# Attention scores from stacked queries and doubled keys, and other ties for row sums and splits, in a decoder trunk kernel

## The chip, the core and the metric

The kernel runs on one core of one Trainium2 chip. Its time is device microseconds, as the median of a few runs; smaller is better. Time before the change: 688.33 us, median of three runs (688.19 to 689.62).

## What is computed

One decoder layer over 512 tokens of 1024 channels, in fp32: an adaLN-modulated RMSNorm, a combined input projection, two causal token mixers (sliding-window attention with 8 query heads on 2 key heads, differential attention with 4 heads of two maps), their branch projections, gates, an output projection, and a gated MLP with a small convolution. The change touches the scores of the two mixers:

```python
qb = q.reshape(b, nb, BLOCK, SWA_KV_HEADS, SWA_GROUP, d)
scores = jnp.einsum('bnqkgd,bnskd->bnkgqs', qb, kb).astype(jnp.float32) * (d ** -0.5)   # sliding window
...
scores = jnp.einsum('bqhmd,bshmd->bhmqs', qblk, k).astype(jnp.float32) * scale          # differential
...
mod = cs @ w_ada[l] + b_ada[l]      # adaLN: shift, scale, gate, twice
```

A head has 64 channels, so a score sums over 64.

## The kernel before

**Split operands.** TensorE (PE) multiplies numbers in the type fp32r. To keep fp32 accuracy each operand is held as a high part (rounded to fp32r by a ScalarE, ACT, copy) and a low part (the rest, by a VectorE, DVE, subtraction): `split` (L101), `split_pair` (L95) for weights, `evac` (L404) for a projection that leaves PSUM. A product is three products: high by high, high by low, low by high (`mm3`, L105). A weight goes through a raw buffer (`raw_tile`, L90, four of them, shared by everything that is loaded so) and a ring of three split buffers (`WB`).

**Scores.** The two sub-heads that are worked on together (two key heads of the window, two maps of a differential head) lie in partitions 0 to 63 and 64 to 127 of the same tile. Their scores are three products each over half of the array's rows, written pairwise by `mm3_rows` (L110): `swa_scores` (L500) for a pair of window heads and two 128-query blocks, `diff_scores` (L609) for one or two blocks of a differential head. The key width is 128 or 256 in the window and 128 to 512 in the differential head. A DVE instruction then adds the distance penalty and takes the row maximum (L527, L634), the softmax runs on ACT and DVE (`swa_softmax` L533, `diff_softmax` L640), and PE transposes the probabilities (`swa_transpose` L553, `diff_transpose` L657) before it multiplies them by the values.

**Order.** In attention the order of PE is written out by hand (`manual_schedule` at L450). Between the pieces of attention `fill(n)` (L459) issues n steps of other projections; a step is three products of 512 columns and a unit has eight or four. `prefetch` (L454) loads and splits the weights of the next units. `fill` also counts ticks, and at the ticks in `ADA_AT` (L30) it takes one row of `ada_rows` (L706): load 128 rows of `w_ada`, and on DVE multiply and sum them (L711) into `late_mod`. There are 32 such rows; the first eight columns feed the gate of the output projection, the others later parts. `issue_after(x)` puts instructions behind x on x's engine, without a wait of their own. The row sums stand behind the last score reduction (`behind_dve`). On DVE and ACT a planner orders the instructions by priority; `high_priority` lifts the softmax.

**Before and after attention.** The first projection sums over eight slices k (`mm_k`, L347) into eight PSUM banks: key (0), window queries 0 and 1 (1, 2), window value (5), values (3, 4, 6, 7). The last slice takes all eight first products, then the other two of each. After attention come the gates and branch products (`add_gate_d` L860, `add_merge` L869, whose weight pairs `wbd` share one buffer, L874), the output projection with rows `wo` (`load_rows` L930, L966), and the MLP, whose first weights are split early (`prep` L1038, L1055).

Of the kernel before, what the change touches and what calls it, by code (L numbers as in the profile page):

```python
# [29 lines left out]
ADA_AT = set(range(20, 150, 8)) | set(range(180, 300, 5))  # L30
# [3 lines left out]
SWA_FILL = (0, 3, 6, 2, 2, 2, 2, 3)  # L34
# [7 lines left out]
def kernel(  # L42
# [50 lines left out]
    lows = [None]  # L93

    def split_pair(raw, shape, name):  # L95
        hi = wp.tile(shape, F32R, tag="whi", bufs=WB, name=name + "_h")
        lo = wp.tile(shape, F32R, tag="wlo", bufs=WB, name=name + "_l")
        lows[0] = split(hi, lo, raw)
        return hi, lo

    def split(hi, lo, src):  # L101
        nc.scalar.copy(hi, src)
        return nc.vector.tensor_sub(lo, src, hi.bitcast(F32))
# [5 lines left out]

    def mm3_rows(groups):  # L110
        for a, b, start, stop in ((0, 0, True, False), (0, 1, False, False), (1, 0, False, True)):
            for o, lhs, rhs in groups:
                nc.tensor.matmul(o, lhs[a], rhs[b], start=start, stop=stop)  # L113
# [233 lines left out]
    def mm_k(k, part):  # L347
# [53 lines left out]
    ka = big.tile([P, 2, S], F32R, tag="kvA", name="ka")  # L401
    outa = [big.tile([P, 4, S], F32R, tag=f"out{g}", name=f"outa{g}") for g in "hl"]

    def evac(hi, lo, src, scale=None):  # L404
        if scale is None:
            nc.scalar.copy(hi, src)
            return nc.vector.tensor_sub(lo, src, hi.bitcast(F32))
# [16 lines left out]

    keep_v(3)
    evac(qa[:, 1, 0], qa[:, 1, 1], acc[2], qsc[:, 1:2])
    keep_v(4)
    nc.scalar.copy(vaT, acc[5])
# [23 lines left out]
    current, tick, behind_dve = [], [0], [None]  # L452
# [6 lines left out]
    def fill(n):  # L459
        for _ in range(n):  # L460
# [20 lines left out]
            if tick[0] in ADA_AT:  # L481
# [18 lines left out]
    def swa_scores(i, n0):  # L500
# [9 lines left out]
        sps = [sbank(f"sw{i}_{n0}_{j}", (P, 2, 256)) for j in range(2)]  # L510
        for n in (n0, n0 + 1):
# [11 lines left out]
        for n in (n0, n0 + 1):  # L523
# [1248 lines left out]
```

## Time and profile before

| | before |
|---|---|
| median of three runs | 688.33 us |
| the profiled execution | 686.36 us |
| its span, first to last instruction | 684.6 us |
| PE busy | 673.5 us |
| PE weight loads busy | 589.6 us |
| DVE busy | 556.8 us |
| ACT busy | 383.5 us |
| GpSimd (POOL) busy | 65.9 us |
| granted TensorE clock | 0.998 |

A line of the timeline reads: start in us, duration in us, engine, line, operation, output and inputs, shapes, count; in square brackets the idle time of the engine before it and what ended it. A matmul's shape gives first the part of the array that it uses (128*128 or 64*128). A matmul's duration holds its way through the array; matmuls overlap, so the cost of one in a sequence is the distance from its start to the next start. PEld is the load of the weights of a matmul. In the chain of work the times are those distances, with a count. SPq is the queue that issues most DMAs. In the list of waits a line gives the total, the number of times and the longest.

### The profile page before, as it was taken

How to read it: one execution, taken by the hardware profiler on the slowest of the kernel's cores; microseconds unless marked ns; L12 is line 12 of the kernel's file. 1: busy time of each engine (PE TensorE's matmuls, PEld its weight loads, DVE VectorE, ACT ScalarE, POOL GpSimd, SP SyncE). 2: the span in 40 equal slices, each digit the busy share in tenths (PEclk: the TensorE clock that was granted, in tenths of full speed). 3: DMA queues.
4: the chain of work that ended last, by engine and by line, in shares of the span. 5: the costliest groups of instructions: out<-in, count | busy, mean ns of one | idle time of the engine just before them, and what ended most of it. 6: DMA issues, size and time to landing. Idle time of an engine off the chain costs nothing.

```text
span 684.6 us, 10929 instructions
## 1 busy us (share of the span) xinstructions
PE 673.5 (98%) x4117; PEld 589.6 (86%) x4117; DVE 556.8 (81%) x1036; ACT 383.5 (56%) x678; POOL 65.9 (10%) x74
## 2 busy tenths in 40 slices
PE   8999999999999999999999999999999999999995
PEld 7887777778788888788799999999999998888884
DVE  5996867778775677773689998888888999979997
ACT  6676756454554332441588565666555666656665
POOL 2000000000100000000020110111110003540300
PEclk9999999999999999999999999999999999999999
DMA  9952224454363667347672989787866658996903
GB/s 355 417 214 79 94 85 149 145 170 150 97 183 94 200 236 245 119 161 226 197 124 83 215 226 209 177 200 186 204 170 184 152 171 198 199 204 187 165 1 124
DMA packets 71077, 119.68 MB, mean 175 GB/s; under 512 B 3952, under 2 KB 47728, under 8 KB 71024
## 3 DMA queue, kind: packets, MB, share of 16 engines
q1 hardware_dynamic: 52960, 95.04, 41.8%
q0 software_dynamic: 17776, 23.60, 21.1%
q8 instruction: 32, 0.52, 0.3%
q10 hardware_dynamic: 288, 0.34, 0.2%
q14 instruction: 21, 0.17, 0.1%
HBM read 116.87 MB, written 2.10 MB: 174 GB/s over the span
## 4 chain that ended last, share of the span: by engine, by line
PE 78%; DMA 9%; DVE 8%; issue 3%; ACT 1%; DVEq 0%; POOLq 0%; ACTq 0%
PE up L1098 32%; PE dc L1701 11%; DMA ra<-in_w_ada_t_dram 4%; PE av L345 3%; DMA s_t<-in_w_up_dram 2%; PE pga L106 2%; PE aqa L342 2%; PE pga L107 2%; PE pga L108 2%; PE sd L113 1%; PE pk L106 1%; PE pq L106 1%; DVE ra L711 1%; PE pk L108 1%; PE pq L108 1%
## 5 line engine op out<-in xcount | busy, mean ns | idle before, releaser
L1098 PE MATMUL up<-t,m_whi 128*128 128x256 f32 x512 | 93.1, 283 | 0.0
L1098 PEld LDWEIGHTS up<-t,m_whi 128*128 128x128 f32 x512 | 79.9, 192 | 0.0
L1098 PE MATMUL up<-t,m_wlo 128*128 128x256 f32 x256 | 72.4, 283 | 0.0
L1098 PE MATMUL up<-bh,p_whi 128*128 128x256 f32 x232 | 65.7, 283 | 0.0
L1098 PE MATMUL up<-bl,p_whi 128*128 128x256 f32 x232 | 65.7, 283 | 0.0
L1098 PE MATMUL up<-bh,p_wlo 128*128 128x256 f32 x232 | 65.7, 283 | 0.0
L711 DVE CUSTOM_DVE_ANT_0 ra<-ra,csb 128x1024 f32<-128x1024 f32 x32 | 39.0, 1220 | 16.5 <-DMA ra<-in_w_ada_t_dram 16.5
L1098 PEld LDWEIGHTS up<-t,m_wlo 128*128 128x128 f32 x256 | 49.2, 192 | 0.0
L1098 PEld LDWEIGHTS up<-bh,p_whi 128*128 128x128 f32 x232 | 44.5, 192 | 0.0
L1098 PEld LDWEIGHTS up<-bl,p_whi 128*128 128x128 f32 x232 | 44.5, 192 | 0.0
L1098 PEld LDWEIGHTS up<-bh,p_wlo 128*128 128x128 f32 x232 | 44.5, 192 | 0.0
L1004 POOL DMA_DIRECT2D s<-in_w_up_dram x21 | 27.0, 1365 | 158.1 <-DMA s<-in_w_up_dram 128.9
L1032 ACT CAST m_whi<-s 128x1024 fp32r<-128x1024 f32 x31 | 32.5, 1048 | 15.7 <-DVE s L1026 9.1
L1036 DVE TENSOR_TENSOR m_wlo<-s,m_whi 128x1024 fp32r<-128x1024 f32 x31 | 37.7, 1217 | 1.3 <-ACT m_whi L1032 1.3
L1098 PE MATMUL up<-t,p_whi 128*128 128x256 f32 x176 | 32.2, 283 | 0.0
L648 ACT ACTIVATE sd<-sd,dmx 128x128 f32<-128x128 f32 (+3 forms) x32 | 17.8, 557 | 23.9 <-DVE dmx L646 23.2
L1098 PEld LDWEIGHTS up<-t,p_whi 128*128 128x128 f32 x176 | 27.4, 192 | 0.1
L144 POOL TENSOR_TENSOR r<-ms,mhalf 128x4 f32<-128x4 f32 x4 | 5.1, 1276 | 219.1 <-DVE dls L652 149.6
L1032 ACT CAST p_whi<-wa 128x1024 fp32r<-128x1024 f32 x18 | 18.8, 1043 | 12.6 <-PE up L1098 9.0
L1036 DVE TENSOR_TENSOR p_wlo<-wa,p_whi 128x1024 fp32r<-128x1024 f32 x18 | 22.0, 1222 | 4.0 <-ACT p_whi L1032 3.3
L1105 ACT ACTIVATE gT<-a,cols 128x512 f32<-128x512 f32 x22 | 17.6, 813 | 13.3 <-DVE a L1140 13.0
L1098 PE MATMUL up<-t,p_wlo 128*128 128x256 f32 x88 | 24.9, 283 | 0.0
(517 smaller groups left out, 2018.8 us busy)
## 6 DMA issues: line engine op xcount, KB each, us to landing
ra<-in_w_ada_t_dram SPq DMA_DIRECT2D x32, 512.0 KB, 3.4
wa<-in_w_up_dram SPq DMA_DIRECT2D x22, 512.0 KB, 4.4
s<-in_w_up_dram SPq DMA_DIRECT2D x21, 512.0 KB, 4.6
s<-in_w_up_dram POOLq DMA_DIRECT2D x21, 512.0 KB, 6.6
adaw<-in_w_ada_t_dram SPq DMA_DIRECT2D x15, 512.0 KB, 9.6
a<-in_w_up_dram SPq DMA_DIRECT2D x11, 512.0 KB, 4.9
b<-in_w_down_dram SPq DMA_DIRECT2D x10, 512.0 KB, 4.1
w<-in_w_first_dram SPq DMA_DIRECT2D x8, 512.0 KB, 9.9
```

The source lines that it names most:

```text
L106: nc.tensor.matmul(o, lh, rh, start=start, stop=False)
L107: nc.tensor.matmul(o, lh, rl, start=False, stop=False)
L108: nc.tensor.matmul(o, ll, rh, start=False, stop=stop)
L345: nc.tensor.matmul(acc[i], ht[:, t : t + P], wts[k][w][:, S:], start=start, stop=stop)
L648: nc.scalar.activation(pm[m], pm[m], AF.Exp, bias=mx[:, m : m + 1], scale=slope, accum_out=lsum[:, m : m + 1])
L711: nc.vector.tensor_tensor_reduce(r, r, csb, 1.0, 0.0, ALU.mult, ALU.add, late_mod[:, idx : idx + 1])
L1004: nc.gpsimd.dma_start(dst, upblock(*blk), accum_op=ALU.add)
L1032: nc.scalar.copy(W[J, name][0], R[J, SRC[name]])
L1036: nc.vector.tensor_sub(lo, R[J, SRC[name]], hi.bitcast(F32))
L1098: nc.tensor.matmul(o[u], w[:, k, cu], b[:, k], start=name in ("p1", "m5", "p2") and k == 0 and x == 0, stop=k == 3 and x == 2, skip_group_ ...
L1105: nc.scalar.activation(grow(j), av[J][:, u], AF.Identity, bias=cv[:, 66 + j : 67 + j], scale=cv[:, 44 + j : 45 + j])
L1701: nc.tensor.matmul((bank2[u] if o is None else o)[:, sl], a[:, q, cu], b[:, q, sl], start=first_mm and x == 0, stop=last_mm and x == 2, sk ...
```

## The change

Queries are stacked: for each sub-head one tile of 128 partitions holds the high part in the sub-head's own 64 partitions and the low part in the other 64. Keys are doubled: the high part in both halves of one tile, the low part in both halves of another. A score is then two products over all 128 rows: stacked query by doubled high key, and by doubled low key. (The sum gains low by low, which the three products left out.) The scores are written sub-head by sub-head.

Beside that: the last slice of the first projection finishes its banks one after the other, value 3 and key first; the order of ACT and DVE right behind it is written out by hand; one filler step comes ahead of the first scores and two, not three, behind them; the value transposes come four filler steps later. The row sums of `ada_rows` no longer come at ticks 20 to 148 but behind the last instruction of a softmax (`ada_behind`), and from tick 180 on at every fifth tick behind the last two splits (`recent`). `wbd` alternates between two buffers. The first `wo` row stands behind the last two splits, and the early split of `p2` behind the last `wo` split on ACT too.

```diff
-ADA_AT = set(range(20, 150, 8)) | set(range(180, 300, 5))
+ADA_LATE = 180
+ADA_EVERY = 5
...
-SWA_FILL = (0, 3, 6, 2, 2, 2, 2, 3)
+VA_AT = 5
+SWA_FILL = (1, 2, 6, 2, 2, 2, 2, 3)
...
+    casts, lows, recent = [None], [None], [None, None]
...
-        lows[0] = split(hi, lo, raw)
+        casts[0], lows[0] = split(hi, lo, raw)
+        recent[:] = recent[1:] + lows
...
-
-    def mm3_rows(groups):
-        for a, b, start, stop in ((0, 0, True, False), (0, 1, False, False), (1, 0, False, True)):
-            for o, lhs, rhs in groups:
-                nc.tensor.matmul(o, lhs[a], rhs[b], start=start, stop=stop)
...
         elif part == 0:
-            for i in range(8):
-                product(k, i, 0)
-        elif part == 1:
-            for i in range(8):
-                product(k, i, 1)
-                product(k, i, 2)
+            for i in (3, 0, 1, 5, 2, 4, 6, 7):
+                for p in range(3):
+                    product(k, i, p)
...
-    ka = big.tile([P, 2, S], F32R, tag="kvA", name="ka")
+    ka = big.tile([P, 2, 2, S], F32R, tag="kvA", name="ka")
+    lower, upper = slice(0, 64), slice(64, P)
...
-    def evac_q(i):
-        evac(qa[:, i, 0], qa[:, i, 1], acc6[i], qsc[:, i : i + 1])
-
-    evac(ka[:, 0], ka[:, 1], acc[0])
-    evac(qa[:, 0, 0], qa[:, 0, 1], acc[1], qsc[:, 0:1])
+    halves = ((lower, upper), (upper, lower))
+
+    def stack(dst, src, scale, js=(0, 1), soon=True):
+        with tc.high_priority(offset=HP) if soon else ExitStack():
+            sc = [scale if isinstance(scale, float) else scale[own] for own, _ in halves]
+            for j in js:
+                own = halves[j][0]
+                nc.scalar.activation(dst[own, j], src[own], AF.Copy, scale=sc[j])
+            for j in js:
+                own, other = halves[j]
+                nc.vector.scalar_tensor_tensor(
+                    dst[other, j], src[own], sc[j], dst[own, j].bitcast(F32), ALU.mult, ALU.subtract
+                )
+
+    def double(dst, src):
+        with tc.high_priority(offset=HP):
+            for j, (own, _) in enumerate(halves):
+                nc.scalar.copy(dst[own, j, 0], src[own])
+            for j, (own, _) in enumerate(halves):
+                nc.vector.tensor_sub(dst[own, j, 1], src[own], dst[own, j, 0].bitcast(F32))
+            for j, (own, other) in enumerate(halves):
+                nc.scalar.copy(dst[other, j], dst[own, j])
...
+    man = ExitStack()
+    man.enter_context(tc.manual_schedule(engines={nc.vector.engine, nc.scalar.engine}))
     keep_v(3)
-    evac(qa[:, 1, 0], qa[:, 1, 1], acc[2], qsc[:, 1:2])
+    for j, (own, other) in enumerate(halves):
+        for to in (own, other):
+            nc.scalar.copy(ka[to, j, 0], acc[0][own])
+    for j, (own, _) in enumerate(halves):
+        nc.vector.tensor_sub(ka[own, j, 1], acc[0][own], ka[own, j, 0].bitcast(F32))
+    stack(qa[:, 0], acc[1], qsc[:, 0:1])
+    for j, (own, other) in enumerate(halves):
+        nc.scalar.copy(ka[other, j, 1], ka[own, j, 1])
+    nc.scalar.copy(vaT, acc[5])
+    man.close()
+    stack(qa[:, 1], acc[2], qsc[:, 1:2], soon=False)
     keep_v(4)
-    nc.scalar.copy(vaT, acc[5])
     keep_v(6)
     keep_v(7)
...
-    current, tick, behind_dve = [], [0], [None]
...
-            if tick[0] in ADA_AT:
+            if tick[0] >= ADA_LATE and tick[0] % ADA_EVERY == 0:
                 next(ada, None)
...
+        sps = {j: sbank(f"sw{i}_{n0}_{j}", (P, 2, 256)) for j in range(2)}
+        for j, n in ((j, n) for j in range(2) for n in (n0, n0 + 1)):
             w = P if n == 0 else 2 * P
             k0 = max(0, n - 1) * P
             qs, ks = slice(n * P, (n + 1) * P), slice(k0, k0 + w)
-            mm3_rows([
-                (
-                    sps[j][:, n - n0, :w],
-                    [qa[64 * j : 64 * j + 64, i, b, qs] for b in range(2)],
-                    [ka[64 * j : 64 * j + 64, b, ks] for b in range(2)],
-                )
-                for j in range(2)
-            ])
-        for n in (n0, n0 + 1):
-            w = P if n == 0 else 2 * P
-            for j in range(2):
+            for b in range(2):
+                nc.tensor.matmul(sps[j][:, n - n0, :w], qa[:, i, j, qs], ka[:, j, b, ks], start=b == 0, stop=b == 1)
+        for j in range(2):
+            for n in (n0, n0 + 1):
+                w = P if n == 0 else 2 * P
...
-                    behind_dve[0] = c.last
...
-                    nc.vector.tensor_scalar_mul(c.sb[n][:, j, :w], c.sb[n][:, j, :w], c.lsum[:, j, n : n + 1])
+                    c.end = nc.vector.tensor_scalar_mul(c.sb[n][:, j, :w], c.sb[n][:, j, :w], c.lsum[:, j, n : n + 1])
...
-            evac(qa[:, i, 0], qa[:, i, 1], o, qsc[:, i : i + 1])
+            stack(qa[:, i], o, qsc[:, i : i + 1])
...
-            t = heads[h] = ap.tile([P, 4, S], F32R, tag="qk", bufs=2, name=f"qk{h}")
+            t = heads[h] = ap.tile([P, 6, S], F32R, tag="qk", bufs=2, name=f"qk{h}")
...
-            evac(t[:, 0], t[:, 1], o, 2.0 ** (2 * h - 1))
+            stack(t[:, 0:2], o, 2.0 ** (2 * h - 1))
...
-            evac(t[:, 2], t[:, 3], o)
+            double(t[:, 2:6].rearrange("p (j b) s -> p j b s", b=2), o)
...
-            mm3_rows([
-                (
-                    sps[m],
-                    [t[64 * m : 64 * m + 64, b, n * P : (n + 1) * P] for b in range(2)],
-                    [t[64 * m : 64 * m + 64, 2 + b, :w] for b in range(2)],
-                )
-                for m in range(2)
-            ])
+            for m in range(2):
+                for b in range(2):
+                    nc.tensor.matmul(
+                        sps[m], t[:, m, n * P : (n + 1) * P], t[:, 2 + 2 * m + b, :w], start=b == 0, stop=b == 1
+                    )
...
-                    behind_dve[0] = nc.vector.tensor_tensor_reduce(
+                    nc.vector.tensor_tensor_reduce(
...
-            nc.vector.scalar_tensor_tensor(pm[0], pm[0], lsum[:, 0:1], pm[1], ALU.mult, ALU.add)
+            end = nc.vector.scalar_tensor_tensor(pm[0], pm[0], lsum[:, 0:1], pm[1], ALU.mult, ALU.add)
             probs[s] = pm[0]
+        return end
...
         with tc.high_priority(offset=HP):
-            end = evac(hi, lo, tp[:, : (n + 1) * P].rearrange("p (k q) -> p k q", q=P))
-        if s == 4 * DIFF_HEADS - 1:
-            behind_dve[0] = end
+            evac(hi, lo, tp[:, : (n + 1) * P].rearrange("p (k q) -> p k q", q=P))
...
+    def ada_behind(op):
+        behind_dve[:] = [op]
+        next(ada)
+        behind_dve.clear()
...
             r = raw_tile([P, D], f"ra{idx}")
             nc.sync.dma_start(r, w_ada_t[2 * D + idx * P : 2 * D + (idx + 1) * P, :])
-            with tc.high_priority(offset=HP // 2), tc.issue_after(behind_dve[0].ins):
+            with ExitStack() as place:
+                place.enter_context(tc.high_priority(offset=HP // 2))
+                for b in behind_dve or recent:
+                    place.enter_context(tc.issue_after(b.ins))
                 nc.vector.tensor_tensor_reduce(r, r, csb, 1.0, 0.0, ALU.mult, ALU.add, late_mod[:, idx : idx + 1])
...
-        fill(1)
+        fill(VA_AT)
         turn_va()
-        fill(SWA_FILL[2] - 1)
+        fill(SWA_FILL[2] - VA_AT)
...
         if more:
             swa_softmax(i + 1)
+            ada_behind(pairs[i + 1].end)
...
         for z in nxt:
-            diff_softmax(z)
+            end = diff_softmax(z)
+        if nxt:
+            ada_behind(end)
...
-                wb = gpart(3, [P, 2, 4, 2 * P], f"wbd{j}", F32R)
+                if j % 4:
+                    wb = bp.tile([P, 2, 4, 2 * P], F32R, tag="m5w", name=f"wbd{j}")
+                else:
+                    wb = gpart(3, [P, 2, 4, 2 * P], f"wbd{j}", F32R)
                 wh, wl = wb[:, 0], wb[:, 1]
-                split(wh, wl, r)
+                casts[0], lows[0] = split(wh, wl, r)
+                recent[:] = recent[1:] + lows
...
-    wo = [load_rows(wout, k, f"wo{k}", g1b) for k in range(KT)]
+    with tc.issue_after(recent[0].ins), tc.issue_after(recent[1].ins):
+        wo = [load_rows(wout, 0, "wo0", g1b)]
+    wo += [load_rows(wout, k, f"wo{k}", g1b) for k in range(1, KT)]
...
+    wo_cast, wo_low = casts[0], lows[0]
     for i, name in enumerate(("p1", "p2")):
-        with tc.issue_after(wo_low.ins) if i else ExitStack():
+        with ExitStack() as behind_wo:
+            if i:
+                behind_wo.enter_context(tc.issue_after(wo_cast.ins))
+                behind_wo.enter_context(tc.issue_after(wo_low.ins))
             early_low = prep(0, name, (early_w[i][:, 0], early_w[i][:, 1]))
```

More of the change, by code (lines that the diff above doesn't have):

```diff
@@ L97, in split_pair @@
         lo = wp.tile(shape, F32R, tag="wlo", bufs=WB, name=name + "_l")
-        lows[0] = split(hi, lo, raw)
+        casts[0], lows[0] = split(hi, lo, raw)
+        recent[:] = recent[1:] + lows
         return hi, lo
     def split(hi, lo, src):
-        nc.scalar.copy(hi, src)
-        return nc.vector.tensor_sub(lo, src, hi.bitcast(F32))
+        return nc.scalar.copy(hi, src), nc.vector.tensor_sub(lo, src, hi.bitcast(F32))
     def mm3(o, lh, ll, rh, rl, start, stop):
@@ L406, in evac @@
             nc.scalar.copy(hi, src)
-            return nc.vector.tensor_sub(lo, src, hi.bitcast(F32))
+            nc.vector.tensor_sub(lo, src, hi.bitcast(F32))
         else:
@@ L451 @@
     units, loaded, later = [], [], []
-    current, tick, behind_dve = [], [0], [None]
+    current, tick, behind_dve = [], [0], []
     def prefetch(most=2):
@@ L509, in swa_scores @@
         c = pairs[i]
-        sps = [sbank(f"sw{i}_{n0}_{j}", (P, 2, 256)) for j in range(2)]
-        for n in (n0, n0 + 1):
+        sps = {j: sbank(f"sw{i}_{n0}_{j}", (P, 2, 256)) for j in range(2)}
+        for j, n in ((j, n) for j in range(2) for n in (n0, n0 + 1)):
             w = P if n == 0 else 2 * P
@@ L933, in load_rows @@
         nc.vector.tensor_mul(r, r, gate)
-        pair = split_pair(r, [P, D], name)
-        return pair
+        return split_pair(r, [P, D], name)
     def tok_proj(acc, lh, ll, wts, nk, done, half_done=None):
@@ L1040, in prep @@
             W[J, name] = dst
-            return split(dst[0], dst[1], R[J, SRC[name]])
+            return split(dst[0], dst[1], R[J, SRC[name]])[1]
         if name in ("m6", "p3"):
```

3 lines of the change are left out of this document (removed).

## Prediction

> **What bounds the kernel now.** The page first: who is busy, and when.
>
> ```profile
> PE 673.5 (98%) x4117; PEld 589.6 (86%) x4117; DVE 556.8 (81%) x1036; ACT 383.5 (56%) x678; POOL 65.9 (10%) x74
> ...
> PE   8999999999999999999999999999999999999995
> ```
>
> TensorE is at nine tenths in all but the first and the last slice. A busy PE is not yet a bound, so the list of who waited for whom, cut to PE, comes next. It names six waits; four lie in the first 16 us, before the change. These two are left:
>
> ```profile
> PE oc L1155 <- DVE wo_l L103: 0.8, 1, 0.8
> ...
> PE pB L108 <- DVE wbd L103: 0.4, 1, 0.4
> ```
>
> So from 16 us on the time is the sum of the distances at which PE starts its products. VectorE and ScalarE matter only where they make PE wait. I therefore price the change in start-to-start distances on PE, and then ask of each other engine whether its new work reaches PE.
>
> **The scores, term 1.** One score group of sliding-window pair 2, in the timeline:
>
> ```profile
> 81.01 0.39 PE L107 MATMUL pq<-hTlA,w_h 128*128 128x512 f32 x1
> ...
> 81.23 0.39 PE L108 MATMUL pq<-hThA,w_l 128*128 128x512 f32 x1
> ...
> 81.55 0.96 PE L113 MATMUL sw<-ka,qa 64*128 64x128 f32 x12
> ...
> 82.44 0.50 PE L106 MATMUL pq<-hThA,w_h 128*128 128x512 f32 x1
> ...
> 82.78 0.39 PE L107 MATMUL pq<-hTlA,w_h 128*128 128x512 f32 x1
> ```
>
> A full 512-wide product follows the one before after 0.22 to 0.23 us (81.01 to 81.23; I use 0.227). The group's first product comes 0.32 us after its predecessor, 0.09 too much. The group takes 0.89 us. The first full product behind it keeps the next waiting 0.34 us, 0.11 too much. So the group costs 82.78 - 81.23 - 2 x 0.227 = 1.10 us, of which 0.20 is neither side's arithmetic: it is paid on entering and leaving the half-array shape. The chain of work gives the other sizes, and the price of full products:
>
> ```profile
> 70.93 0.77 PE tp L562 x7
> ...
> 87.02 0.91 PE sw L113 x12
> ...
> 124.05 0.72 PE sd L113 x6
> ...
> 129.33 0.90 PE sd L113 x6
> ...
> 356.06 216.11 PE up L1098 x1800
> ```
>
> ```profile
> 144.41 0.34 PE L107 MATMUL od<-aTl,vvh 128*128 128x384 f32 x1
> ...
> 144.59 0.33 PE L108 MATMUL od<-aTh,vvl 128*128 128x384 f32 x1
> ```
>
> Full-array prices: 128 wide 0.77/7 = 0.110 us, 256 wide 216.11/1800 = 0.120, 384 wide 0.18 (144.41 to 144.59; 0.175 taken), 512 wide 0.227. The chain counts a group from its first start to the next full product's, so 0.20 is added to each of its rows.
> - Blocks 0 and 1 (12 halves, 128 and 256 wide): 1.10 now. After: 4 x 0.110 + 4 x 0.120 = 0.92. Saves 0.18, in 4 sliding-window and 4 differential groups: 1.44.
> - Blocks 2 and 3 of the window (12 halves of 256): 0.91 + 0.20 = 1.11, after 8 x 0.120 = 0.96. Saves 0.15 x 4 = 0.60.
> - 384 wide (6 halves): 0.72 + 0.20 = 0.92, after 4 x 0.175 = 0.70. Saves 0.22 x 4 = 0.88.
> - 512 wide: 0.90 + 0.20 = 1.10, after 4 x 0.227 = 0.91. Saves 0.19 x 4 = 0.76.
>
> Term 1 is **-3.7 us**. No row shows a 128-row product that loads one weight twice running, nor a score group in full shape. The bounds: the bodies alone (0.89 against 0.92, 0.91 against 0.96, 0.72 against 0.70, 0.90 against 0.91) give +0.4 if the 0.20 stays, and -4.5 if the second load of a weight were spared about 0.01 us a product at 128 products (no row decides that, the gap between the 128- and 256-wide price is 0.01). I take -3.7, since product groups of unlike width already follow each other above at plain distances.
>
> The Trainium skill, "TensorEngine Tiling (Array Packing)", section Key Properties, says that changing the tiling mode, not just the tile, drains TensorE; the 0.20 us agree. Its page "TensorE: Matmul & The Clock Gate", section Part 3, speaks against the change: products on different row groups run concurrently, so three pairs of halves should cost three full products where the new code pays four. That is a rival below.
>
> **The operands, on ScalarE and VectorE.** Queries are split twice over 64 partitions, keys twice, and keys copied once more to the other 64.
>
> ```profile
> L113 PE MATMUL sd<-qk x96: 268/328/498, 115.3 to 205.8; 64*128 64x128 f32 x24, 64*128 64x256 f32 x24, 64*128 64x384 f32 x24, 64*128 64x512 f32 x24
> ...
> L410 DVE SCALAR_TENSOR_TENSOR qk<-pq,qk x4: 660/682/692, 91.1 to 172.6; 128x512 fp32r<-128x512 f32 x4
> L406 ACT CAST qk<-pk x4: 567/583/600, 96.6 to 179.1; 128x512 fp32r<-128x512 f32 x4
> ```
>
> An instruction's time goes by its 512 columns; halving its partitions I price at nothing saved (bounds: half, or nothing). A head's query adds 0.58 us on ACT and 0.68 on DVE, its key 0.58 + 2 x 1.05 (two 1024-column copies, like the cast at 329.41 below) on ACT and 0.68 on DVE. Four heads: 13 us ACT, 5.5 DVE. Four window queries and the window key add some 5.4 us ACT and 3.4 DVE. All lies beside products; the page's 56% and 81% have room. The heads' keys are needed late: head 0's are split from 96.6 on, its scores start at 115.3. The crowded place is the first stretch:
>
> ```profile
> 56.00:80.00 24.00, 24.00 (x152) 18.56 (x152) 19.88 (x71) 16.02 (x50) 0.00 (x0) 1.00 0.28 91
> ```
>
> DVE is busy 19.9 of 24 us there; four splits of 0.7 bring it to 22.7. At its front:
>
> ```profile
> 56.47 0.59 ACT L406 CAST ka<-aka 128x512 fp32r<-128x512 f32 x1 [1.21 <-PE aka L342]
> ...
> 56.99 1.27 ACT L409 ACTIVATE qa<-aqa,qsc 128x512 fp32r<-128x512 f32 x2
> ...
> 57.78 1.41 DVE L410 SCALAR_TENSOR_TENSOR qa<-aqa,qsc,qa 128x512 fp32r<-128x512 f32 x2
> ...
> 59.22 0.39 PE L345 MATMUL av<-whi,hTlB 128*128 128x512 f32 x1
> ```
>
> The last projection product starts at 59.22. With each group of three together, keys finish 18 products earlier (59.22 - 18 x 0.227 + 0.39 = 55.5), query 0 at 56.2. ACT then has nine instructions in a written order before the scores have all their operands: about 9 x 0.55 = 5 us from 55.2, so 60.2. PE asks after one filler step, at 59.45 + 0.68 = 60.1. That nearly meets. The second score group, 0.92 + 1.36 later at 62.4, needs the bank that query 1 leaves; its pair of splits (1.27 ACT, then DVE) ends between 62 and 63.5. I take a **+0.5 us** stall (bounds 0 and 1.8).
>
> **The row sums, inside attention.** Sums of adaLN rows now follow a softmax's last instruction, 14 of them (3 window, 11 differential), not a score reduction.
>
> ```profile
> 138.85 1.22 DVE L711 CUSTOM_DVE_ANT_0 ra<-ra,csb 128x1024 f32<-128x1024 f32 x1
> ...
> 142.90 0.35 DVE L654 SCALAR_TENSOR_TENSOR sd<-sd,dls,sd 128x128 f32<-128x128 f32 x1
> ...
> 142.92 0.39 PE L108 MATMUL pk<-hThA,w_l 128*128 128x512 f32 x1
> ...
> 143.40 0.30 PE L663 MATMUL td<-ident,sd 128*128 128x128 f32 x1
> ```
>
> Here a sum of 1.22 us sits inside the softmax that PE is about to wait for: the transpose starts 0.48 us after a product, 0.25 late. The new tie takes it out; the added splits use the same engines. I take **-0.2** (bounds -0.5, if a second transpose like it is freed too, and +3, 1 us for each of three heads).
>
> **The ties of the splits, terms 2 and 3.** First the branch weights:
>
> ```profile
> 273.08 1.05 ACT L102 CAST wgd_h<-wgd 128x1024 fp32r<-128x1024 f32 x1 [1.62 <-DMA wgd<-in_w_tiles_dram]
> ...
> 274.52 1.04 ACT L102 CAST wbd<-wbd 128x1024 fp32r<-128x1024 f32 x1
> ...
> 275.91 1.23 DVE L933 TENSOR_TENSOR wo<-wo,g1b 128x1024 f32<-128x1024 f32 x1 [0.52 <-DMA wo<-in_w_out_dram]
> ...
> 277.65 1.22 DVE L103 TENSOR_TENSOR wbd<-wbd,wbd 128x1024 fp32r<-128x1024 f32 x1
> ...
> 278.09 0.39 PE L107 MATMUL pB<-vvl,wbd 128*128 128x512 f32 x1
> ...
> 278.92 0.50 PE L108 MATMUL pB<-vvh,wbd 128*128 128x512 f32 x1 [0.44 <-DVE wbd L103]
> ```
>
> The wbd subtraction stands behind the first output weight's multiplication, which waited for its DMA. PE loses 0.83 - 0.23 = 0.60. The change puts that multiplication behind the last two splits, and alternates wbd between two buffers, so the split no longer waits for PE. I take **-0.6** (bounds 0 and -0.6). Then the last output weight:
>
> ```profile
> 328.07 0.61 PE L1158 MATMUL oc<-wo_h,mg2l 128*128 128x512 f32 x2
> ...
> 329.41 1.05 ACT L102 CAST early<-wa 128x1024 fp32r<-128x1024 f32 x1 [1.09 <-DMA wa<-in_w_up_dram]
> ...
> 330.36 1.05 ACT L102 CAST wo_h<-wo 128x1024 fp32r<-128x1024 f32 x1
> ...
> 331.46 0.50 PE L1154 MATMUL oc<-wo_h,mg3h 128*128 128x512 f32 x1
> ...
> 332.72 0.50 PE L1155 MATMUL oc<-wo_l,mg3h 128*128 128x512 f32 x1 [0.76 <-DVE wo_l L103]
> ```
>
> PE loses 1.26 - 0.23 = 1.03. Its buffer is free at 328.68, yet ACT first waits for the early cast's DMA. The new tie puts that cast behind the last wo cast: 328.7 + 1.05 + 1.23 = 331.0, before PE's 331.46. I take **-1.0** (bounds 0 and -1.0). The early cast's weight is used from about 348 on, so 1 us later costs nothing.
>
> **Sum.** -3.7 + 0.5 - 0.2 - 0.6 - 1.0 = -5.0 us. The profiled execution took 686.36 us (span 684.6), so 681.4 for it; the median of the runs, 688.33, stands 1.97 above, so **683.3**.
>
> **Rivals.**
> - *Crowding takes it back.* The differential transpose at 143.40 starts 0.15 us after its input (142.90 + 0.35). If the doubled keys' 2.7 us of ACT work get ahead of a softmax in each head, about 1 us per head is lost, and 1.3 more at the start: 683.3 + 3 to 5 = 686 to 688. For: DVE at 22.7 of 24. Against: most slack is larger, and a sum of 1.22 leaves the chain.
> - *The change doesn't do what it says:* full score groups keep a gap as large as the 0.20. Then term 1 is +0.4 and the time 687.4. Against: every full-shape sequence above goes at plain distances.
> - *Halves are concurrent, and cheaper.* Three pairs at full-product price against four products adds one product per block: 4 x (0.110 + 3 x 0.120) + 4 x (0.110 + 0.120 + 0.175 + 0.227) = 4.4 us, and 683.3 + 3.7 + 4.4 = 691.4. The row at 81.55 refuses it: 0.89 for the group, not 0.69.
> - *Slower: row sums hold the ring of raw buffers.* After tick 180 each of 18 sums now stands behind the last two splits, which themselves wait for DMAs.
>
> ```profile
> L711 DVE CUSTOM_DVE_ANT_0 ra<-ra,csb 128x1024 f32<-128x1024 f32 x32 | 39.0, 1220 | 16.5 <-DMA ra<-in_w_ada_t_dram 16.5
> ```
>
> DVE already idles 16.5 us before them. The sums share four buffers with the weights. The weight cast at 273.08 serves products that start 8 us later (277.87 + 12 x 0.227 + 0.6 = 281.2). If each sum holds a buffer 4 us longer, 18 x 4 / 4 = 18 us of the ring go; past the 8 us of lead PE waits 10: 693. It decides once a sum's hold grows by 8 x 4 / 18 = 1.8 us. Against: nothing waits on the sums until the ring is dry, and the splits' buffers come free a unit ahead.
>
> **Chances.** Forecast 0.62 (681.3 to 685), crowding 0.18, no gain in shape 0.07, concurrent halves 0.02, ring 0.11 (688 to 693, as lead is eaten). Range 681.0 to 688.0: below lie 0.05, above about 0.15. A measurement of this kernel tells 0.2%, 1.4 us, from no change. Faster: 0.62 + 0.11 of crowding + 0.05 = 0.78; slower: 0.02 + 0.09 = 0.11; same 0.11.
>
> **What would show it.** Right: score groups with full products 0.11 to 0.23 us apart and no longer distance around them; no PE wait on wbd nor wo_l; DVE and ACT busy some 9 and 18 us more; the up stage's x1800 unchanged but about 5 us earlier. Wrong: a PE wait between 60 and 64 us or at td transposes over 1 us; PE waiting for wgd between 215 and 300 us; full score products at 0.15 us or more for 256 columns.

## The result and the profile after

| | before | after |
|---|---|---|
| median beside each other | 688.87 us (687.87 to 689.62, 8 runs) | 684.62 us (683.12 to 687.55, 8 runs) |
| ratio, 95% interval | | 0.9953 [0.9932, 0.9973] (the medians alone give 0.9938) |
| in a later session | 688.59 us | 683.64 us, ratio 0.9929 [0.9915, 0.9944] |
| the profiled execution and its span | 686.36, 684.6 us | 684.12, 682.3 us |

The change makes the kernel faster: by 0.3 to 0.7% in the first session, by 0.6 to 0.9% in the later one, 4 to 5 us by the medians. The forecast was 683.3. The sum came out near; several of its terms did not, in opposite directions, and the experiments below separate them. Some executions show a lower granted clock (0.991 to 0.995 against 0.996 to 0.998) and are longer, which lifts a median that holds many of them, and none of them was profiled: three of eight of the changed kernel here (687.1 to 687.6 us against 683.1 to 684.9), six of twelve of the half-array products below (691.4 to 695.1 against 688.3 to 690.0), eight of twelve of the weight ties alone (medians 689.0 against 687.5).

First the page of the changed kernel, the line of busy time, and from the groups the row sums:

```profile
PE 670.2 (98%) x4053; PEld 594.3 (87%) x4053; DVE 567.7 (83%) x1049; ACT 403.7 (59%) x703; POOL 66.1 (10%) x74
```

```profile
L732 DVE CUSTOM_DVE_ANT_0 ra<-ra,csb 128x1024 f32<-128x1024 f32 x32 | 38.6, 1221 | 1.6 <-DMA ra<-in_w_ada_t_dram 1.5
```

DVE has 10.9 us more work and ACT 20.2, where 9 and 18 were expected. The idle time of DVE ahead of the row sums fell from 16.5 us to 1.6: they hardly wait for their loads any more.

The waits of PE in the changed kernel (total, times, longest, in us):

```profile
PE oc L1186 <- DVE tdall L913: 1.3, 1, 1.3
...
PE sw L540 <- DVE mx L545: 0.5, 1, 0.5
PE pqa L110 <- DVE wqa_l L105: 0.4, 1, 0.4
...
PE sw L540 <- DVE qa L418: 0.2, 1, 0.2
```

The waits for wbd and for wo_l are gone. Four others stand in their place: three at the start of attention and one, the largest, for the last merge (the DVE step that takes a branch product out of its PSUM bank).

**A score group now**, in the timeline:

```profile
82.58 0.39 PE L110 MATMUL pq<-hThA,w_l 128*128 128x512 f32 x1
82.80 1.08 PE L540 MATMUL sw<-ka,qa 128*128 128x128 f32 x8
83.72 0.40 PE L108 MATMUL pq<-hThA,w_h 128*128 128x512 f32 x1
83.96 0.39 PE L109 MATMUL pq<-hTlA,w_h 128*128 128x512 f32 x1
```

0.22 us in, 0.92 for the group, 0.24 to the next: plain distances on both sides, as forecast. The chain of work gives the other groups and the up stage:

```profile
115.97 1.11 PE sd L637 x8
124.81 0.71 PE sd L637 x4
129.88 0.91 PE sd L637 x4
...
154.11 1.03 PE sd L637 x4
...
353.73 216.13 PE up L1130 x1800
```

0.71 and 0.91 are the forecast's 0.70 and 0.91. But 1.11 (blocks 0 and 1 of the first differential head) and 1.03 (512 wide, in three heads of four) are longer than 0.92 and 0.91. The timeline shows who stands in front of them:

```profile
114.71 1.25 PE L590 MATMUL oa<-pT,va 128*64 128x256 f32 x12
115.89 1.18 PE L637 MATMUL sd<-qk 128*128 128x128 f32 x8
116.91 0.40 PE L108 MATMUL pga<-hThA,wga_h 128*128 128x512 f32 x1
```

```profile
153.17 0.95 PE L701 MATMUL pss<-ones,sq 128*128 128x1 f32 x8
153.97 1.17 PE L637 MATMUL sd<-qk 128*128 128x512 f32 x4
154.99 0.39 PE L108 MATMUL pga<-hThA,wga_h 128*128 128x512 f32 x1
```

The first follows products of another shape of the array (128*64). The three others follow products of one column (128x1), which use the full shape, so that there the shape of the array does not change. In both places the group takes 1.02 us (115.89 to 116.91, 153.97 to 154.99), about 0.1 more than in the plain places.

**The start of attention.**

```profile
59.46 0.39 PE L110 MATMUL pqa<-hThA,wqa_l 128*128 128x512 f32 x1
...
59.87 0.72 PE L540 MATMUL sw<-ka,qa 128*128 128x128 f32 x4
...
60.75 0.70 PE L540 MATMUL sw<-ka,qa 128*128 128x128 f32 x4 [0.15 <-DVE qa L418]
...
61.29 0.40 PE L108 MATMUL pqa<-hThA,wqa_h 128*128 128x512 f32 x1
...
62.32 0.74 DVE L418 SCALAR_TENSOR_TENSOR qa<-aqa,qsc,qa 64x512 fp32r<-64x512 f32 x1 [0.93 <-ACT qa L415]
62.44 0.39 PE L110 MATMUL pqa<-hThA,wqa_l 128*128 128x512 f32 x1
62.66 0.63 PE L540 MATMUL sw<-ka,qa 128*128 128x256 f32 x4
63.08 0.29 DVE L545 CUSTOM_DVE_ANT_0 st<-sw,dsw 128x128 f32<-128x128 f32 x1
...
63.78 0.74 PE L540 MATMUL sw<-ka,qa 128*128 128x256 f32 x4 [0.48 <-DVE mx L545]
64.36 0.40 PE L108 MATMUL pqa<-hThA,wqa_h 128*128 128x512 f32 x1
```

Without a stall the first group's successor would start at 59.46 + 0.23 + 0.92 = 60.61; it starts at 61.29, 0.68 late. The second's would start at 62.44 + 0.23 + 0.96 = 63.63; it starts at 64.36, 0.73 late. DVE does query 1's low part (62.32) ahead of the reductions (63.08) whose bank the second group needs. A third stall follows:

```profile
68.46 0.40 PE L109 MATMUL pqa<-hTlA,wqa_h 128*128 128x512 f32 x1
...
69.24 0.50 PE L110 MATMUL pqa<-hThA,wqa_l 128*128 128x512 f32 x1 [0.39 <-DVE wqa_l L105]
```

0.78 - 0.23 = 0.55. The three make 1.96 us. Two smaller late starts come on top: the product behind the third stall starts 0.34 us later in place of 0.23, and the score group at 74.84 takes 1.27 us, where the like group of the fastest version below takes 1.04. The start costs some 2.3 us in all.

**The last merge.**

```profile
301.16 0.61 PE L1190 MATMUL oc<-wo_h,mg0l 128*128 128x512 f32 x2
301.24 1.23 DVE L961 TENSOR_TENSOR wo<-wo,g1b 128x1024 f32<-128x1024 f32 x1 [0.64 <-DMA wo<-in_w_out_dram]
302.39 0.68 DVE L913 SCALAR_TENSOR_TENSOR tdall<-tdall,pB 128x512 f32<-128x512 f32 x1
...
303.12 0.50 PE L1186 MATMUL oc<-wo_h,mg0h 128*128 128x512 f32 x1 [1.34 <-DVE tdall L913]
```

The merge frees a bank that PE needs. It stands on DVE behind an output weight's multiplication, and that one waited for its DMA. PE loses 303.12 - 301.16 - 2 x 0.23 = 1.5 us.

### The profile page after: what moved, and what is told of

It reads as the page before. It is cut to its first block, busy times and chain, and to the rows that moved or that the text cites. A ratio compares the mean times of both kernels' runs of the same rounds, so it can differ in the third digit from the quotient of the medians.

```text
span 682.3 us, 10835 instructions
## 1 busy us (share of the span) xinstructions
PE 670.2 (98%) x4053; PEld 594.3 (87%) x4053; DVE 567.7 (83%) x1049; ACT 403.7 (59%) x703; POOL 66.1 (10%) x74
## 4 chain that ended last, share of the span: by engine, by line
PE 79%; DVE 8%; DMA 6%; issue 3%; ACT 3%; ACTq 0%; DVEq 0%
PE up L1130 33%; PE dc L1733 11%; DMA wgd<-in_w_tiles_dram 3%; PE av L342 3%; DMA wo<-in_w_out_dram 2%; PE oc L1186 2%; PE oc L1187 2%; PE oc L1190 2%; PE pga L108 2%; PE pga L110 2%; PE pga L109 2%; PE sd L637 2%; PE aqa L339 1%; PE pq L108 1%; PE pk L108 1%
## 5 line engine op out<-in xcount | busy, mean ns | idle before, releaser
L662 ACT ACTIVATE sd<-sd,dmx 128x128 f32<-128x128 f32 (+3 forms) x32 | 17.8, 557 | 20.7 <-DVE dmx L660 16.5
```

The lines of the kernel that those rows point to most:

```text
L662: nc.scalar.activation(pm[m], pm[m], AF.Exp, bias=mx[:, m : m + 1], scale=slope, accum_out=lsum[:, m : m + 1])
```

## Experiments

Three sessions, each on one chip with its own runs of the kernel before (medians 688.32, 688.59 and 688.34 us): the first four experiments, the next four, the rest. Milestones are first starts on PE in the timelines: first sw, last od (the end of attention), first up.

### A second profile of the kernel before

No edit.

> The kernel before once more, for a second profile. The first profiled execution, 686.36 us, lies 2.5 us below the median of its runs. If executions differ at one place, this profile shows it as a PE wait or a late start that the first has not, of about 2 us; if they differ everywhere a little, no single distance on PE is over 0.3 us longer.

688.77 us, span 687.0. The forecast's profile had been a short execution (686.36). In the timeline:

```profile
277.55 1.23 DVE L933 TENSOR_TENSOR wo<-wo,g1b 128x1024 f32<-128x1024 f32 x1 [1.39 <-DMA wo<-in_w_out_dram]
...
280.56 0.50 PE L108 MATMUL pB<-vvh,wbd 128*128 128x512 f32 x1 [1.80 <-DVE wbd L103]
```

It is the same queue as at 275.91 in the forecast, but the multiplication can start 1.6 us later and PE loses 1.96, not 0.60; an earlier wbd wait of 0.50 comes on top. This table sets the two profiles of each kernel side by side:

| us | before, 1st | before, 2nd | after, 1st | after, 2nd |
|---|---|---|---|---|
| first sw to last od | 158.21 | 158.40 | 156.23 | 156.24 |
| last od to first up | 130.38 | 132.97 | 129.70 | 128.96 |
| first up to the end | 336.46 | 336.64 | 336.46 | 336.42 |

Attention repeats within 0.2 us; the stretch that is fed by DMA differs by 2.6 us in one and the same kernel. One filler step (0.68) has moved ahead of the first sw, so at equal work attention gained 1.3 to 1.5 us. Behind it the gain is 0.7 by the first pair of profiles and 4.0 by the second. The time ahead of attention varies too: the first product of the projection, where all versions are alike, starts between 15.05 and 15.87 us in the profiles of this document.

### The other ties alone

The kernel before with all of the changed ties (row sums, wbd, first wo row, p2), scores as before.

```diff
-            if tick[0] in ADA_AT:
+            if tick[0] >= ADA_LATE and tick[0] % ADA_EVERY == 0:
...
+            ada_behind(pairs[i + 1].end)
...
+                if j % 4:
+                    wb = bp.tile([P, 2, 4, 2 * P], F32R, tag="m5w", name=f"wbd{j}")
...
+    with tc.issue_after(recent[0].ins), tc.issue_after(recent[1].ins):
+        wo = [load_rows(wout, 0, "wo0", g1b)]
...
```

> The kernel before with only the other ties: row sums behind the softmax and behind the last two splits, two buffers for the branch weights, the first output row behind the last splits, the early split behind the last output cast. Scores, operand splits and the start of attention are those of before. Theory: PE's waits on wbd (0.6 us) and on the last wo_l (1.0 us) go, the late transposes of the differential heads (0.45 us in all) too, and the new wait of the output projection for the last merge (1.5 us) comes with them: 0.5 to 2.2 us faster than before, 686.7 to 688.4. Rival (the ties carry the gain): 684 to 685.5.

684.77 us, ratio 0.9953 [0.9938, 0.9969]: the rival held. The ties alone bring as much as the whole change did in its first runs (0.9953), and about 1 us less than it did in the later session (683.64 us, 0.9929). The profile shows where: the waits for wbd and wo_l are gone, and 1.23 us (by distance) are lost to the last merge instead.

### The scores alone

The changed kernel with the row sums, wbd, wo and p2 placed as before.

```diff
-            ada_behind(pairs[i + 1].end)
...
-                if j % 4:
-                    wb = bp.tile([P, 2, 4, 2 * P], F32R, tag="m5w", name=f"wbd{j}")
-                else:
-                    wb = gpart(3, [P, 2, 4, 2 * P], f"wbd{j}", F32R)
+                wb = gpart(3, [P, 2, 4, 2 * P], f"wbd{j}", F32R)
...
```

> The changed kernel's scores, operand splits, last projection slice and start of attention, with the row sums, branch weights and output rows tied as before. Theory: the score groups give 2.9 us, the crowded start takes 1.7 to 2 of them back, and the waits on wbd and wo_l stay: 0.5 to 1.5 us faster than before, 687.4 to 688.4. Rival (the scores carry the whole gain): 684 to 685.5. Second rival (row sums inside the softmax, with the added splits, make PE wait at each differential head): slower than before, 690 or more.

688.26 us, ratio 1.0007 [0.9993, 1.0021]: within the range that was expected and no gain that is clear of the noise, but for another reason than only the start. PE's waits include:

```profile
PE pB L109 <- DVE wbd L104: 1.2, 2, 0.7
...
PE td L678 <- DVE dls L665: 0.6, 1, 0.6
PE td L678 <- DVE sd L668: 0.6, 1, 0.6
```

The differential transposes now wait twice. The timeline names what stands in their softmax:

```profile
119.52 1.22 DVE L731 CUSTOM_DVE_ANT_0 ra<-ra,csb 128x1024 f32<-128x1024 f32 x1
...
123.80 0.74 DVE L668 SCALAR_TENSOR_TENSOR sd<-sd,dls,sd 128x128 f32<-128x128 f32 x2
...
124.20 0.33 PE L678 MATMUL td<-ident,sd 128*128 128x128 f32 x1 [0.56 <-DVE sd L668]
```

A row sum of 1.22 us sits between the score reductions and the end of the softmax, as one did at 138.85 in the kernel before. The changed kernel has two weight splits of 1.2 us on DVE in this stretch; here the same two stand behind the row sum, and PE waits. From the first sw to the last od this kernel takes 158.19 us. One filler step (0.68) lies ahead of its first sw, so at equal work that is about 0.6 us more than in the kernel before, although its score groups are those of the changed kernel. With the row sums behind the softmax (the changed kernel) it is 156.24: that tie is worth 1.95 us once the scores are full products. By distances 0.68 and 0.80 of it are the two transposes, and 0.32 is a third late product.

### Half-array products from the new operands

The changed kernel with three half-array products a score, high by low taken twice in place of low by high.

```diff
-            for b in range(2):
-                nc.tensor.matmul(sps[j][:, n - n0, :w], qa[:, i, j, qs], ka[:, j, b, ks], start=b == 0, stop=b == 1)
+            for x, b in enumerate((0, 1, 1)):
+                for j in range(2):
+                    own = halves[j][0]
+                    nc.tensor.matmul(
+                        sps[j][:, n - n0, :w], qa[own, i, j, qs], ka[own, j, b, ks], start=x == 0, stop=x == 2
+                    )
```

> The changed kernel with all its new splits and ties, but each score again as three products over half of the array, from the same stacked and doubled tiles (high by high, high by low, and high by low once more in place of low by high, so the scores lack the low queries). Theory (the gain of the scores is the array's shape, paid on entering and leaving it): each score group again has about 0.09 us too much ahead of it and 0.11 behind it, the groups together cost 2.5 to 3.5 us more than in the changed kernel, and the time is 687 to 688.5. Rival (the shape costs nothing, the gain is in the ties): the time stays within 1 us of the changed kernel's 684.6.

690.72 us, ratio 1.0037 [1.0017, 1.0057]. By the runs at a clock of 0.996 and more it is 688.9 us against 684.1 for the changed kernel, so the half products cost 4.7 us, where 2.5 to 3.5 were expected. The waits of PE show why it is not a clean measure of the shape:

```profile
PE sw L542 <- DVE qa L418: 1.4, 2, 0.8
...
PE tp L583 <- ACT va L460: 0.7, 1, 0.7
```

The start stalls grow with it, from 1.96 to 0.90 + 0.95 + 0.72 + 0.91 = 3.5 us by distances.

### The last two output weights behind the last merge

```diff
+            merged[0] = nc.vector.scalar_tensor_tensor(td, td, 1.0, o, ALU.add, ALU.mult)
...
+    wo += [load_rows(wout, k, f"wo{k}", g1b) for k in range(1, 6)]
+    with tc.issue_after(merged[0].ins):
+        wo += [load_rows(wout, k, f"wo{k}", g1b) for k in range(6, KT)]
```

> The changed kernel with one more tie: the last two output rows' multiplications stand on VectorE behind the last merge's first instruction. In the changed kernel the sixth row's multiplication waits for its DMA until 301.2 us with the merge behind it, and PE waits 1.5 us for the merge. Theory: that wait goes and nothing takes its place: 1.3 to 1.5 us faster than the changed kernel, about 683.2. Rival (the next thing is late anyway, the early weights or the output rows): within 0.5 us of the changed kernel.

682.7 us, ratio 0.9916 [0.9902, 0.993], against 683.64 for the changed kernel beside it. Its profile still has a wait of 0.65 us for the merge (by distance), with another cause:

```profile
297.08 1.23 DVE L963 TENSOR_TENSOR wo<-wo,g1b 128x1024 f32<-128x1024 f32 x1 [1.39 <-DMA wo<-in_w_out_dram]
...
302.06 0.68 DVE L915 SCALAR_TENSOR_TENSOR tdall<-tdall,pB 128x512 f32<-128x512 f32 x1
```

The row ahead of the two came late, and the last merge still stands behind it on DVE. This profile is of the longest of the six runs (683.62 us; the others 682.3 to 683.0), so it does not show where the runs gain 0.9 us.

### Query 1 and the last values behind the first reductions

```diff
-    stack(qa[:, 1], acc[2], qsc[:, 1:2], soon=False)
-    keep_v(4)
-    keep_v(6)
-    keep_v(7)
...
     with tc.issue_after(pairs[0].last.ins):
+        stack(qa[:, 1], acc[2], qsc[:, 1:2], soon=False)
+        keep_v(4)
         fill(SWA_FILL[1])
         swa_scores(0, 2)
+    with tc.issue_after(lows[0].ins):
+        keep_v(6)
+        keep_v(7)
```

> The changed kernel with another order on VectorE at the start of attention: query 1's splits behind the first score group's reductions, and the splits of values 6 and 7 behind the second filler weight's. No work is left out. Theory (the start's 1.7 us are an order, not a full engine): the PE waits at 63.0 us (0.64) and 68.5 us (0.56) go, some 0.5 to 1.2 us faster than the changed kernel. Rival (VectorE is simply full there): the waits move to the following transposes or units and the time stays within 0.4 us.

682.92 us, ratio 0.9919 [0.9903, 0.9936], 0.7 below the changed kernel; the intervals overlap, so the times alone do not show it. The profiles do: from the first sw to the last od it is 155.54 us, against 156.23 and 156.24. The second and third stall are gone, and a new one has come at the value transposes, 1.00 us by distance:

```profile
PE pva L455 <- DVE lsum L560: 0.8, 1, 0.8
```

### Both of these

Both edits together.

> The two edits together: merge before the last output rows, and the other order at the start. Theory: the gains add, 1.8 to 2.7 us faster than the changed kernel, 682 to 682.8. Rival: as much as the better one alone.

681.77 us, ratio 0.9903 [0.9888, 0.9918]. All five runs (681.57 to 682.34) lie below all six of the changed kernel beside them (683.13 to 684.64). It is the fastest version, 1.9 us below the changed kernel; the wait for the last merge is gone.

### The changed kernel beside them

No edit.

> The changed kernel again beside the three, on the same chip: 684.6 us, ratio 0.994 to before. Its eight runs so far fall into five at 683.1 to 684.9 and three at 687.1 to 687.6. If this second profile is one of the long ones it shows at which place 3 us are lost; a PE wait for a DMA is what I expect.

683.64 us, ratio 0.9929 [0.9915, 0.9944]. Its wait for the last merge is 0.73 us by distance, against 1.5 in the first profile.

### The row sums alone, and the weight ties alone

The ties of the second experiment, taken apart. First the row sums:

```diff
-            if tick[0] in ADA_AT:
+            if tick[0] >= ADA_LATE and tick[0] % ADA_EVERY == 0:
...
+                for b in behind_dve or recent:
+                    place.enter_context(tc.issue_after(b.ins))
```

> The kernel before with one of the ties alone: the row sums stand behind the last instruction of a softmax and, from tick 180 on, behind the last two splits. Theory (the gain of the ties is the branch-weight wait and the output-weight wait, and the row sums are worth next to nothing): 687.5 to 689.0, no difference from before, with the branch-weight wait of 0.6 to 2.5 us and the last output weight's wait of 1.0 us still there. Rival (taking the sums out of the softmax is what gains): 685 to 686.5, with both of those waits unchanged.

686.72 us, ratio 0.9982 [0.9972, 0.9992]. Neither theory's numbers: more than nothing, less than the rival's, and by neither's way. The transpose that the forecast named is as late as before, and one other (at 193.94 us in the kernel before) starts 0.20 us earlier. What went is the wbd wait:

```profile
273.53 1.22 DVE L104 TENSOR_TENSOR wbd<-wbd,wbd 128x1024 fp32r<-128x1024 f32 x1
...
274.66 1.22 DVE L718 CUSTOM_DVE_ANT_0 ra<-ra,csb 128x1024 f32<-128x1024 f32 x1
```

Row sums that are put off fill this stretch. The first wo load is issued at 284.78 us, not at 271.97 as before, so its multiplication no longer stands ahead of the wbd split. PE then waits for the last output weight, 0.70 and 1.03 us by distance (0.21 and 1.03 in the kernel before).

The weight ties:

```diff
-                wb = gpart(3, [P, 2, 4, 2 * P], f"wbd{j}", F32R)
+                if j % 4:
+                    wb = bp.tile([P, 2, 4, 2 * P], F32R, tag="m5w", name=f"wbd{j}")
...
+    with tc.issue_after(recent[0].ins), tc.issue_after(recent[1].ins):
+        wo = [load_rows(wout, 0, "wo0", g1b)]
...
+                behind_wo.enter_context(tc.issue_after(wo_cast.ins))
...
```

> The kernel before with the other ties alone: the branch weights in two buffers in turn, the first output weight behind the last two splits, the early split behind the last output weight's cast; the row sums stay as before. Theory: 684.7 to 686, 3 us below before, since the branch-weight wait (0.60 in one profile of the kernel before, 2.46 in the other) and the last output weight's wait (1.0) go, and about 1 us comes back as a wait for the last merge. Rival (the row sums carry it): 687 to 688.5.

688.67 us, ratio 1.0004 [0.9994, 1.0015]: my theory fell. The waits for wbd and wo_l do go, but this comes:

```profile
306.32 1.04 ACT L103 CAST m5w<-s_t 128x1024 fp32r<-128x1024 f32 x1 [6.45 <-DMA s_t<-in_w_up_dram]
307.27 1.07 ACT L858 COPY g2row<-pg 128x512 f32<-128x512 f32 x2
...
307.90 0.50 PE L1169 MATMUL oc<-wo_h,mg0h 128*128 128x512 f32 x1 [2.42 <-ACT g2row L858]
```

ACT stands at a cast whose weight lands at 306.3; the copy that frees PE's next bank is queued behind it. PE loses 2.6 us there and 0.4 at the merge. In the changed kernel the same cast runs at 299.78 with no wait. Neither tie holds the gain alone: the row sums bring 0.2%, the weight ties 0 to 0.1%, together they bring 0.5%. The late weight is issued at 297.51 us and takes 8.7 us with the weight ties alone, at 292.68 and 6.6 in the changed kernel; why it is issued so much later there, no run takes apart.

### All ties and the merge, and half products with both orders

The ties alone with the edit of the last merge.

> The kernel before with all of the ties and the last two output weights behind the last merge's first instruction, scores as before. Theory: 0.5 to 1.5 us below the ties alone, 683.3 to 684.3, since the wait for the last merge (1.2 us there) goes; the kernel with both orders, whose scores are full products, stands another 1.7 to 2.5 us lower, which is what the full products are worth when their own start costs little. Rival (the full products are worth nothing with the ties in place): as fast as the kernel with both orders, 681.8.

683.99 us, ratio 0.9949 [0.9934, 0.9963], no wait of PE behind attention left. In its profile and that of the kernel with both orders, the stretches behind attention are equal: 128.02 us each from the last od to the first up, 336.44 from there to the end. All that differs is ahead of it: the first sd starts 0.46 us earlier (115.50 and 115.04), and from there to the last od it is 102.44 against 100.30. That makes 2.60 us, but 0.82 of it lies ahead of the first product of the projection (15.87 and 15.05 us), where the two kernels are alike. So the new scores, with the better start, are worth **1.8 us** by these two profiles; the medians, of two sessions, differ by 2.2. No run takes the new order of the last projection slice and the moved filler steps alone; these figures hold them too.

Then the kernel with both orders, but half-array products.

> The kernel with both orders, but every score as three products over half of the array from the same stacked and doubled operands (high by low taken twice in place of low by high). Theory (the shape change costs 0.20 us a group, and the start and transpose stalls cost what they cost in either shape): 2.9 to 3.7 us above the kernel with both orders, 684.7 to 685.5. Rival (half of the distance between the changed kernel and its half-array twin was the shape, the rest stalls that the half products bring about): 5 to 7 us above, with PE waits for queries at 60 to 74 us.

687.08 us, ratio 0.9987 [0.9977, 0.9998], 5 us above, in the rival's range. The profiled execution is one of the longest of its twelve (688.04). The spans differ by 6.5 us; only part of it is the shape:

```profile
83.28 0.39 PE L110 MATMUL pq<-hThA,w_l 128*128 128x512 f32 x1
83.59 0.96 PE L538 MATMUL sw<-ka,qa 64*128 64x128 f32 x12
84.48 0.50 PE L108 MATMUL pq<-hThA,w_h 128*128 128x512 f32 x1
84.82 0.39 PE L109 MATMUL pq<-hTlA,w_h 128*128 128x512 f32 x1
```

84.82 - 83.28 - 2 x 0.227 = 1.09 us; in full shape the like was 83.96 - 82.58 - 2 x 0.227 = 0.93. Summed so over all 20 groups, without the start stalls, the shape is worth 2.9 us (window 1.2, differential 1.6). Another 1.1 is the wait for the last merge, which is back in this profile. 0.9 lies behind the first up, where no score is, 0.6 of it behind the last product; why, stays open. Of the remaining 1.6, 0.2 lies ahead of the first product of the projection and some 1.3 in attention, where the stalls that I can name by distances (start, two transposes) make 0.9.

## Why the forecast was near, step by step

- *Term 1, forecast -3.7:* the mechanism held, the size was -2.9. The step that failed was to save 0.20 us of shape in every group. The first differential group stands behind products of 128*64 and saves nothing (0.97 us in the kernel before, 1.00 now, counted like the 1.10 of the forecast); three 512-wide groups stand behind one-column products and save 0.07 each in place of 0.19. These four make 0.6 of the missing 0.8; the rest is at most 0.03 in each other group. The Trainium skill, "TensorEngine Tiling (Array Packing)", section Key Properties, says that a change of mode drains TensorE; the trace agrees at the first differential group, where the mode changes with full products too. Behind the one-column products the mode does not change; what costs 0.1 us there stays open. The bound of -4.5 does not come out of its own figures: 0.01 us on 64 second products would give -4.3, on 128 products -5.0.
- *The rival of concurrent halves:* The rival by the Trainium skill, "TensorE: Matmul & The Clock Gate", section Part 3 (products on different row groups run concurrently), is refused as a forecast: 12 halves take 0.89 us, eight full products 0.92. The concurrency itself is there: in the 512-wide group at 129.26 us of the kernel before, the two halves of a pair start 0.003 us apart, and the middle pair takes 0.235 us, about as long as one full product. But the first pair takes 0.335 and the last 0.327. So the half shape costs 0.2 us inside the group too, beside the 0.20 at its edges.
- *The start, forecast +0.5, bounds 0 to 1.8:* 1.96, and 2.3 with the two smaller late starts. I had foreseen the second group's stall, but took a part of it. I had not seen that the filler's weight split comes late: on DVE it stands behind three value splits, which run at 66.17 to 68.05 us in the changed kernel. Before, all four value splits ran at 59.11 to 61.58, where the added key and query splits stand now.
- *Row sums in attention, forecast -0.2:* wrong in its reasoning. With the old scores the tie leaves the transpose that I had named as late as it was (0.25 us) and frees another by 0.20; from the first sw to the last od it is 158.15 us, against 158.21 and 158.40. The named transpose is on time in the kernel with the new scores alone, where the row sums are tied as before. With the new scores the tie holds off 1.95 us of new waits. In attention it is hardly a gain by itself, but the cover for the added operand work. The crowding that I gave 0.18 is what happens without it.
- *The wbd wait, forecast -0.6:* the wait went, but 0.6 was a low sample. The second profile has 2.46. This is the largest error of the sum, and it stands twice: the forecast carried the 1.97 us between its short execution and the median over unchanged, while this wait alone makes 1.9 us of difference between the two profiles and is gone in the changed kernel.
- *The last output weight, forecast -1.0:* right at that place, 1.03 in both profiles. What I had not priced is what came in its stead: the wait for the last merge, 0.7 to 1.5 us.
- *Sum:* in attention I expected -3.4 and -1.3 to -1.5 us came. Behind it I expected -1.6 and -0.7 to -4.0 came. The two misses cancelled; that the sum came out near is in part luck.
- *Rivals and signs:* row sums did not hold the ring; their idle time fell to 1.6 us. Score groups kept no gap, except behind other products. One sign of being wrong showed in part, PE waits between 60 and 64 us (0.68 and 0.73 us by distance), and the up stage came 2.3 us earlier by the first profiles, 4.9 by the second, where 5 was expected.

## What to carry to other kernels

Price a change of array shape from the neighbours of each group, not from one group: here nothing was saved behind products of another shape (128*64), and a third of the usual saving behind one-column products. Take a wait that hangs on a DMA from two profiles at least, and read what is queued behind it on each engine, since two ties that each remove a wait were worth 0.2% and next to nothing apart, and 0.5% together. Before two profiles are subtracted, look whether they differ ahead of the first instruction that was changed. A tie that gains little today can be the cover for the work that another edit adds.

## What the runs showed of the hardware

The same load of the first output weight took 3.9 us from issue to landing in one profile of the kernel before (271.97 to 275.88) and 4.5 in the other (272.98 to 277.52). With an issue 1.0 us later that turned a stall of 0.60 us into 1.96, while attention repeated within 0.2 us.

An instruction over 64 partitions cost as much as one over 128: in the changed kernel a subtraction of 64x512 on DVE took 0.69 us (128x512: 0.68), a copy of 64x512 on ACT 0.58 us (128x512: 0.58). That is as the forecast priced it.
